# Pacing the convolution inside an attention: taps tied to sections, a later q chain, an earlier modulation vector

## The chip, the cores and the metric

The kernel runs on one core of a Trainium2 chip. The metric is the device time of one execution in microseconds (us), taken as the median of several runs. TensorE is called PE here, VectorE DVE, ScalarE ACT, GpSimd POOL and SyncE SP; SP issues nearly all DMAs.

## The reference

Two layers of a diffusion trunk, on 128 context and 512 latent tokens of width 1024. The change lies in the mixer of layer 0, which adds an attention (8 heads of 64, 2 key heads) and a convolution branch (512 channels, width 31) before one output projection:

```python
h = modulate(x, mod[0], mod[1])            # mod = silu(c) @ w_ada[l] + b_ada[l], 6 vectors a layer
q, k, v, u = split(h @ w_in)               # q, k: RMS norm, latents also rotated
att = softmax(q k^T) v                     # latents see latents and a cached context
a, gt = split(u); u = a * sigmoid(gt)      # GLU
u = silu(layernorm(depthwise_conv(u, w[31]) + bias))
x = layernorm(alpha * x + mod[2] * (concat(att, u) @ w_out))
# then FFN with mod[3..5]; layer 1 (mLSTM and FFN) likewise
```

## The kernel before

All products are fp32 split into a high and a low part, three matmuls each (L214 to L216). Tokens are 5 tiles of 128: tile 0 is context, 1 to 4 are latents.

**Ahead of the attention** the input projection runs in the order `GEMMS = "01k2qr3"`: GLU units 0 and 1 of the convolution, keys and values, GLU unit 2, two q groups ("q", "r") of four heads, GLU unit 3. Each GLU unit ends in `gated` (sigmoid `sg` on ACT, L1037; product `up` on DVE, L1041) and then `conv(i)`, the 31 taps of its 128 channels into `cy`. A tap is one DVE instruction (L1025), or a multiplication on ACT (L1030) and an addition on POOL (L1032); `CONV_DVE[i]` lists those on DVE. Taps are issued at low priority, so that a scheduler puts them where an engine is free. Each q group ends in a `chain` (L1118 to L1140) on DVE: sum of squares (L1123), some 15 instructions on 128x20 values that make a reciprocal root (L425 to L433), and scaling and rotation of 128x1024 values. Two modulation vectors for layer 0's first step are computed at the very start; `pending` holds generators of further vectors (`ada_vec`). A vector takes eight k-steps, each two loads of 256 KB and matmuls `psc<-whi,stat` and `psc<-wlo,stat`. `background()` advances them by a step. A buffer `ada_m` (L292 clears it on POOL) takes a vector's bias and result.

**The attention** is ordered by hand: 4 pairs of heads of 6 sections each, 24 sections. A section has scores of latents (`ps<-kTA,qT`), their maximum `nm` on DVE (L1218), the exponential on ACT (L1220), transposes on PE, their copies `pT` (DVE, L1266) and the products with the values (`po<-pT,vS`). In each section `modulation()` runs two k-steps of a vector while fewer than `ADA_PAIRS` have been run, and `conv_step()` counts sections (`step`). From step `NORM_AT` = 19 on, four sections in a row advance `conv_norm`: means of half the tokens (PE, then L1345 on DVE), means of the rest, variances (squares L1352 on ACT, 40 matmuls `psc<-ones,csq`, a reciprocal root on DVE), then scaling (`dg` L1368, matmuls `psc<-dg,ones`, L1373). The tanh and the rest of the swish (L1379 to L1386) are issued behind the last section. Pair 2 uses the queries of group "r" through `prep(2)`, in section 6.

**Behind it** comes `out_proj_halves` (L214 to L216), whose first PE row is that at 324.65 us below.

Of the kernel before, what the change touches and what calls it, by code (L numbers as in the profile page):

```python
# [9 lines left out]
F32 = mybir.dt.float32  # L10
# [8 lines left out]
P = 128  # L19
# [37 lines left out]
PS_F1 = (5, 3)  # L57
COMB_WHOLE = True
LATE_DVE = 0
CONV_DVE = (range(31), range(15), range(23, 31), range(8, 31))  # L60
PT_ACT = (4,)
NORM_AT = 19
CN_DVE = (1, 1)
SPLIT0 = None
LATE_AFF = (0, 1, 2, 3, 4)
LATE_LO = ()
PTOK = 8
GEMMS = "01k2qr3"
ADA_IN_ATT = 5
ADA_PAIRS = 20  # L70
FAST = (1, 3)
FIRST_DVE = ()
FIRST_HI = ((0, 0, 0), (0, 0, 1), (0, 1, 0), (0, 1, 1))
# [20 lines left out]
def trunk_kernel(ctx: ExitStack, tc: tile.TileContext, I, O):  # L94
# [17 lines left out]
    K.piece = 0  # L112
    K.pe = None
    K.ordered = False
    K.ada_group = 1
    K.tail = False

# [31 lines left out]
    def ps1(dtype=F32):  # L149
        return K.psB.tile([P, 512], dtype, name="ps1")  # L150
# [83 lines left out]
    adap = ada_scope.enter_context(tc.tile_pool(name="adap", bufs=2, side="right"))  # L234
    psc_scope = ctx.enter_context(ExitStack())
    psC = psc_scope.enter_context(tc.tile_pool(name="psC", bufs=1, space=PSUM, side="right", reuse_waits="tile"))
    K.ada_m = lambda: adap.tile([P, 256], F32, name="ada_m")

    def ring_raw():
        return tuple(f32(x) for x in ring_pair())  # L240
# [92 lines left out]
    def ada_vec(l, v):  # L333
        return ada_steps(l, [(v, 256 * j) for j in range(4)], {2: 0, 5: 1}.get(v))
# [159 lines left out]
    def out_proj_halves(w, S, finish):  # L494

        ah, al = act
        ws = load_n512(w, 0)
        pss = [ps1() for _ in range(NT)]
# [472 lines left out]

    K.startup = False
    K.ada_raw = ring_raw
    pending += [ada_vec(0, v) for v in (2, 3, 4)]

    with ExitStack() as m0s:
        m0 = m0s.enter_context(tc.tile_pool(name="m0", bufs=1, reuse_waits="tile"))
# [12 lines left out]
        if True:  # L990
# [16 lines left out]
                scalar1=0.5, scalar2=None, op0=ALU.mult)  # L1007
            S0 = PAD + SEQ + PAD

            def conv(i):  # L1010

                y = cy[:, i, :]
                with tc.high_priority(offset=-CONV_BEHIND):
                    dve = CONV_DVE[i]
                    if 0 in dve:
                        nc.vector.tensor_scalar(
                            out=y, in0=up[:, i, 0:CW], scalar1=cw[:, i, 0:1], scalar2=cols[:, 64 + i:65 + i],
                            op0=ALU.mult, op1=ALU.add)
                    else:
                        nc.scalar.activation(  # L1020
                            out=y, in_=up[:, i, 0:CW], func=AF.Identity, scale=cw[:, i, 0:1],
                            bias=cols[:, 64 + i:65 + i])
                    for k in range(1, CONV_K):
                        if k in dve:
                            nc.vector.scalar_tensor_tensor(  # L1025
                                out=y, in0=up[:, i, k:k + CW], scalar=cw[:, i, k:k + 1], in1=y,
                                op0=ALU.mult, op1=ALU.add)
                        else:
                            tp = upp.tile([P, CW], F32, name="tap", bufs=2)
                            nc.scalar.activation(  # L1030
                                out=tp, in_=up[:, i, k:k + CW], func=AF.Copy, scale=cw[:, i, k:k + 1])
                            nc.gpsimd.tensor_tensor(out=y, in0=y, in1=tp, op=ALU.add)  # L1032

            def gated(i, half, pa, pg):

# [15 lines left out]
            def glu(i, steps=2):  # L1051
                us = u_w[0] if i == 0 else u_units(i)
                for half in range(2):
                    ps = u_ps[half] if i == 0 else ps2()
                    pa, pg = ps[:, 0], ps[:, 1]
                    ks = range(4, 8) if i == 0 else range(KT)
                    fm_half(us[1], half, pg, ks)
                    fm_half(us[0], half, pa, ks)
                    background(steps)
                    gated(i, half, lambda: pa, pg)  # L1060
                conv(i)

            def glu_behind(i):
                us = u_units(i)
                for half in range(2):
                    pg = psC.tile([P, 512], F32, name="psc")
                    fm_half(us[1], half, pg)

                    def a_part():
                        pa = psC.tile([P, 512], F32, name="psc")  # L1070
                        fm_half(us[0], half, pa)
                        return pa

                    gated(i, half, a_part, pg)
                    yield
                conv(i)


            gains = cvp.tile([P, 2, HD], F32, name="gains")
# [33 lines left out]
            def chain(x, c0, n):  # L1113
# [48 lines left out]
            def q_group(grp, kn=None):  # L1162
                ws = load_n256(w_in, grp * 256)
                for t in range(NT):
# [50 lines left out]
        def exps(ps, dst, sm, multi):  # L1215

            nm = att.tile([P, 1], F32, name="nm", bufs=4)
            nc.vector.tensor_reduce(  # L1218
                out=nm, in_=ps, axis=AX.XY if multi else AX.X, op=ALU.max, negate=True)
            nc.scalar.activation(out=dst, in_=ps, func=AF.Exp, bias=nm[:, 0:1], scale=1.0, accum_out=sm)  # L1220

        def context_weights(i):

            qT, g = qTs[i], i // 2
            sp = ps2()
            pp = Ps[i, -1] = att.tile([P, 2, P], F32, name="pp")
            for h in range(2):
                for x, kT in enumerate((kTA, kTB)):
                    matmul(
# [24 lines left out]
        def turned(i, s, j):  # L1254
# [8 lines left out]
            if j in PT_ACT:  # L1263
                nc.scalar.copy(out=pT, in_=tp)
            else:
                nc.vector.tensor_copy(out=pT, in_=tp)  # L1266
            return pT

        def values(i, s, j, pT):
# [118 lines left out]
        ada_late = [(0, 5)] + [(1, v) for v in range(6)]  # L1388
# [27 lines left out]
        parts = prep(1)  # L1416
        next(parts)
        next_weights(2)
        step, norm = 0, None

        def conv_step():

# [2 lines left out]
            if step == NORM_AT:  # L1425
# [60 lines left out]
        K.ordered = False  # L1486
        K.ada_group = 1
        drain()
        for _ in norm:
            pass  # L1490
        cls.close()
    ada_scope.close()
    psum_plan(0, *PS_F0)
# [82 lines left out]
        nc.sync.dma_start(out=v_d[:, h, t], in_=tmp[:, 0:256])  # L1576

    with Sub(0) as S:
        S.rows(ALPHA)
        out_proj_halves(I["w_out_a"][0], S, S.finish_mixer("f0"))  # L1580
# [526 lines left out]
```

## Time and profile before

| | |
|---|---|
| median of 3 runs | 1729.05 us (1727.44 to 1731.74) |
| profiled execution, own time | 1731.09 us |
| its span | 1729.3 us |
| busy share in the span | PE 92%, DVE 62%, POOL 57%, ACT 46% |
| mean granted PE clock | 0.964 |

The own time is the span with what lies around it. In the rows, the granted clock is a share of full speed: 1.00 is the level of 2.4 GHz, and 0.5 that of 1.2 GHz. `[7.65 <-DVE up L1041]` behind a row means that the engine stood idle for 7.65 us before it, until that instruction ended. A matmul of plain fp32 operands leaves two records in the trace.

### The profile page before, as it was taken

To read this page: it belongs to the slowest core of one execution; us is meant where nothing else is said; L and a number is where in the kernel's file an instruction comes from. 1 tells how busy PE (TensorE), PEld (TensorE's weight loads), DVE (VectorE), ACT (ScalarE), POOL (GpSimd) and SP (SyncE) were. 2 spreads that over 40 slices of the span, in tenths; PEclk is the share of its full clock that TensorE was granted. 3 is DMA by queue.
4 is the path that set the end of the run, shared out by engine and by line. 5 is a ranking of instruction groups with operands and counts; after the bars stand their busy time and mean duration, and the time that the engine had idled before them with its cause. 6 is when DMAs were issued, how large, how long until landed. Compare 5 with 4: busy or idle time off the path is not lost. (4 is left out here: it accounts for less than half of the span.)

```text
span 1729.3 us, 26777 instructions
## 1 busy us (share of the span) xinstructions
PE 1594.5 (92%) x9931; PEld 1403.9 (81%) x9931; DVE 1071.3 (62%) x1840; ACT 798.5 (46%) x1557; POOL 980.6 (57%) x750
## 2 busy tenths in 40 slices
PE   7989689898999999999898998997989999999996
PEld 4679456687879889888788998897988989989885
DVE  2897697477434344456777778688497245344467
ACT  2235765345444344444544545555265444344343
POOL 2346622257746546548656756755459755546555
PEclk9999799798999999999999999998999999999998
DMA  9854475233653212225232322326342422213241
GB/s 304 270 161 133 140 249 149 73 106 117 214 161 101 85 62 98 75 73 195 83 106 81 101 59 88 121 73 203 115 159 79 135 86 91 93 55 98 85 149 71
DMA packets 149257, 211.71 MB, mean 122 GB/s; under 512 B 11845, under 2 KB 88873, under 8 KB 149128
## 3 DMA queue, kind: packets, MB, share of 16 engines
q1 hardware_dynamic: 148896, 209.94, 37.5%
q8 instruction: 78, 1.28, 0.3%
q14 instruction: 51, 0.42, 0.1%
q10 hardware_dynamic: 232, 0.08, 0.0%
HBM read 186.74 MB, written 23.24 MB: 121 GB/s over the span
## 5 line engine op out<-in xcount | busy, mean ns | idle before, releaser
L188 POOL TENSOR_TENSOR wlo<-raw,whi 128x512 fp32r<-128x512 f32 x366 | 503.5, 1396 | 373.2 <-ACT whi L187 367.2
L187 ACT CAST whi<-raw 128x512 fp32r<-128x512 f32 x360 | 220.1, 620 | 405.3 <-PE ps L216 192.9
L214 PE MATMUL ps<-whi,h 128*128 128x512 f32 x640 | 252.2, 396 | 6.1 <-DVE acc L819 2.9
L215 PE MATMUL ps<-wlo,h 128*128 128x512 f32 x640 | 253.7, 397 | 0.0
L216 PE MATMUL ps<-whi,h 128*128 128x512 f32 x640 | 253.3, 396 | 0.0
L215 PE MATMUL ps<-act_l,whi 128*128 128x320 f32 (+2 forms) x704 | 220.1, 313 | 5.8 <-POOL act_l L687 4.2
L214 PE MATMUL ps<-act_h,whi 128*128 128x320 f32 (+2 forms) x704 | 220.0, 315 | 4.8 <-ACT act_h L686 4.5
L216 PE MATMUL ps<-act_h,wlo 128*128 128x320 f32 (+2 forms) x704 | 218.9, 312 | 0.0
L188 POOL TENSOR_TENSOR wlo<-s,whi 128x512 fp32r<-128x512 f32 x118 | 161.6, 1374 | 80.8 <-ACT whi L187 69.7
L819 DVE TENSOR_TENSOR acc<-acc,ps 128x512 f32<-128x512 f32 x120 | 82.0, 685 | 163.5 <-PE ps L216 163.4
L214 PEld LDWEIGHTS ps<-whi,h 128*128 128x128 f32 x640 | 120.7, 189 | 36.1 <-issue 3.8
L216 PEld LDWEIGHTS ps<-whi,h 128*128 128x128 f32 x640 | 120.7, 189 | 28.3
L215 PEld LDWEIGHTS ps<-wlo,h 128*128 128x128 f32 x640 | 120.7, 189 | 27.9 <-issue 0.4
L214 PEld LDWEIGHTS ps<-act_h,whi 128*128 128x128 f32 x704 | 134.1, 191 | 10.8 <-ACT act_h L686 5.2
L215 PEld LDWEIGHTS ps<-act_l,whi 128*128 128x128 f32 x704 | 134.3, 191 | 8.9 <-POOL act_l L687 4.5
L216 PEld LDWEIGHTS ps<-act_h,wlo 128*128 128x128 f32 x704 | 134.3, 191 | 0.0
L214 PE MATMUL ps<-T_h,whi 128*128 128x320 f32 x336 | 104.3, 310 | 3.3 <-ACT pr L611 2.1
L187 ACT CAST whi<-s 128x512 fp32r<-128x512 f32 x120 | 73.3, 615 | 72.0 <-DVE s L562 44.4
L214 PE MATMUL ps<-whi,act_h 128*128 128x256 f32 (+1 forms) x340 | 104.3, 310 | 1.4 <-DVE acc L1155 0.9
L215 PE MATMUL ps<-wlo,act_h 128*128 128x256 f32 (+1 forms) x340 | 104.4, 309 | 0.0
L215 PE MATMUL ps<-T_l,whi 128*128 128x320 f32 x336 | 104.0, 309 | 0.0
L216 PE MATMUL ps<-T_h,wlo 128*128 128x320 f32 x336 | 103.9, 309 | 0.0
(460 smaller groups left out, 3999.8 us busy)
## 6 DMA issues: line engine op xcount, KB each, us to landing
raw<-in_w_ff_dram SPq DMA_DIRECT2D x128, 512.0 KB
whi<-in_w_ada_dram SPq DMA_DIRECT2D x80, 256.0 KB
wlo<-in_w_ada_dram SPq DMA_DIRECT2D x80, 256.0 KB
raw<-in_w_in_m_dram SPq DMA_DIRECT2D x32, 512.0 KB
ada_w<-in_w_ada_dram SPq DMA_DIRECT2D x32, 256.0 KB
acc_d<-acc SPq DMA_DIRECT2D x15, 512.0 KB
raw<-in_w_in_a_dram SPq DMA_DIRECT2D x12, 512.0 KB
rx<-acc_d SPq DMA_DIRECT2D x20, 256.0 KB
```

What stands on the lines that cost most here:

```text
L187: nc.scalar.copy(out=hv, in_=src)
L188: (eng or nc.gpsimd).tensor_tensor(out=lv, in0=src, in1=f32(hv), op=ALU.subtract)
L214: nc.tensor.matmul(out=out, lhsT=lh, rhs=rh, start=start, stop=False)
L215: nc.tensor.matmul(out=out, lhsT=lh, rhs=rl, start=False, stop=False)
L216: nc.tensor.matmul(out=out, lhsT=ll, rhs=rh, start=False, stop=stop)
L819: nc.vector.tensor_tensor(out=x, in0=x, in1=ps, op=ALU.add)
```

## The change

Six edits. (1) `CONV_DVE[3]` becomes `range(16, 31)`: eight taps of unit 3 go from DVE to ACT and POOL. (2) `conv` becomes a generator. The 16 ACT taps of unit 3 are issued three to a section from section 1 on, the remaining DVE taps (8 of unit 2, then 15 of unit 3) three to a section from section 6 on, each ordered behind the latest `nm`, exponential or `pT` copy (`K.anchor`); this is an order on one engine, not a wait between engines. (3) The chain of group "r" moves from the end of its projection into section 1. (4) A third `ada_m` buffer; `pending` takes four vectors ahead of the attention in place of three, and the attention four in place of five (sections 1 to 14 in place of 1 to 18). (5) The four steps of `conv_norm` are taken in sections 16, 17, 19 and 21 in place of 19, 20, 21 and 22. (6) The rows of the gate and norm (`S.rows`) load behind the first half of the output weights.

```diff
-CONV_DVE = (range(31), range(15), range(23, 31), range(8, 31))
+CONV_DVE = (range(31), range(15), range(23, 31), range(16, 31))
-NORM_AT = 19
+NORM_AT = 16
+NORM_STEPS = (16, 17, 19, 21)
+TAPS_AT = 6
+POOL_TAPS = 3
+DVE_TAPS = 3
-ADA_IN_ATT = 5
-ADA_PAIRS = 20
+ADA_IN_ATT = 4
+ADA_PAIRS = 16
...
-    K.ada_m = lambda: adap.tile([P, 256], F32, name="ada_m")
+    K.ada_m = lambda: adap.tile([P, 256], F32, name="ada_m", bufs=3)
...
-    pending += [ada_vec(0, v) for v in (2, 3, 4)]
+    pending += [ada_vec(0, v) for v in (2, 3, 4, 5)]
...
+                            if paced:
+                                behind(ins.ins, K.anchor["act"])
                             nc.gpsimd.tensor_tensor(out=y, in0=y, in1=tp, op=ALU.add)
+                    if paced or (i == 2 and k + 1 in dve):
+                        yield k
+                        paced = True
...
-                nc.vector.tensor_reduce(out=ss, in_=s1v, axis=AX.X, op=ALU.add)
+                ins = nc.vector.tensor_reduce(out=ss, in_=s1v, axis=AX.X, op=ALU.add)
+                if "dve" in K.anchor:
+                    behind(ins.ins, K.anchor["dve"])
...
-                chain(0, grp * 256, 4)
+                if grp == 0:
+                    chain(0, 0, 4)
...
-            if norm is not None and step < NORM_AT + 4:
+            if step in NORM_STEPS:
                 next(norm)
+            if step == 1:
+                chain(0, 256, 4)
+            for _ in range(POOL_TAPS if step < TAPS_AT else DVE_TAPS):
+                if step < TAPS_AT and len(acts) < 16:
+                    acts.append(next(taps[3]))
+                elif step >= TAPS_AT:
+                    if next(taps[2], None) is None:
+                        next(taps[3], None)
```

Three places show how the instructions move. The first is DVE just ahead of the attention's first latent maximum. Before, the end of the chain of group "r" (L1127 to L1140) stands around the last `up` of GLU unit 3:

```order
L1127 TENSOR_TENSOR acc_87<-acc_87,rr4_1839 128x5x256
L1128 TENSOR_TENSOR acc_87<-acc_87,gains_530 128x256
L1131 TENSOR_TENSOR qk_s1_1835<-acc_87,gsin_538 128x256 x4
L1199 TENSOR_TENSOR act_h_89<-acc_87,act_h_89 128x5x64
L1137 TENSOR_TENSOR acc_87<-acc_87,gcos_537 128x4x256
L1199 TENSOR_TENSOR act_h_89<-acc_87,act_h_89 128x5x64
L1041 SCALAR_TENSOR_TENSOR up_519<-sg_1987,ps2_1938 128x320
L1140 TENSOR_TENSOR acc_87<-acc_87,qk_s1_1835 128x4x256
L1218 TENSOR_REDUCE nm_2068<-ps2_2061 128x1
```

In the changed kernel the same stretch, from the first chain's last instruction (L1176) to that maximum (L1255), is:

```order
L1176 TENSOR_TENSOR acc_87<-acc_87,qk_s1_1708 128x4x256
L1236 TENSOR_TENSOR ptok_2028<-acc_87,ptok_2028 128x5x64
L1236 TENSOR_TENSOR ptok_2031<-acc_87,ptok_2031 128x5x64
L1075 SCALAR_TENSOR_TENSOR up_519<-sg_1968,ps2_1919 128x128
L1075 SCALAR_TENSOR_TENSOR up_519<-sg_1968,ps2_1919 128x192
L1236 TENSOR_TENSOR act_h_89<-acc_87,act_h_89 128x5x64 x2
L1075 SCALAR_TENSOR_TENSOR up_519<-sg_2021,ps2_1972 128x320
L1255 TENSOR_REDUCE nm_2057<-ps2_2050 128x1
```

All 24 instructions of the second chain are gone from here; `up` stands behind six short ones only. The second place is DVE in the middle of pair 0. Before, taps (L1025) stand between maxima and copies:

```order
L1218 TENSOR_REDUCE nm_2373<-ps2_2366 128x1
L1025 SCALAR_TENSOR_TENSOR cy_506<-up_519,cw_521,cy_506 128x655
L1235 RECIPROCAL ri_2376<-smc_2372 128x1
L1218 TENSOR_REDUCE nm_2380<-ps2_2366 128x1
L1025 SCALAR_TENSOR_TENSOR cy_506<-up_519,cw_521,cy_506 128x655
L1266 COPY pT_2411<-ps1_2406 128x512
```

Now the second chain's short instructions (L437 to L445) stand there, between the same kinds of neighbours:

```order
L1157 TENSOR_REDUCE ss4_2214<-qk_s1_2212 128x20
L437 TENSOR_SCALAR rh_v_2217<-ss4_2214 128x20
L1304 COPY pT_2259<-ps1_2254 128x512
L438 TENSOR_SCALAR rr4_2216<-rh_v_2217 128x20
L1255 TENSOR_REDUCE nm_2267<-ps2_2261 128x1
L439 TENSOR_SCALAR rr4_2216<-rr4_2216 128x20
L1304 COPY pT_2275<-ps1_2270 128x512
L442 TENSOR_TENSOR rh_a_2218<-rr4_2216 128x20
```

The chain fills sections 1 to 5; one tap is left in pair 0, 15 stand in pair 1 and 7 in pair 2. The third place is PE in section 16, the fourth of pair 2. Before, two k-steps of a modulation vector (`psc_3001<-whi`, `wlo`) stand between context scores and values:

```order
L128 MATMUL ps2_3048<-kTB_504,qT_2816 128x128
L128 MATMUL psc_3001<-whi_3068,stat_109 32x256 x2
L128 MATMUL psc_3001<-wlo_3069,stat_109 32x256 x2
L128 MATMUL psc_3001<-whi_3076,stat_109 32x256 x2
L128 MATMUL psc_3001<-wlo_3077,stat_109 32x256 x2
L128 MATMUL po_2905<-pT_3030,vS_505 64x256 x2
```

Now the first means of the convolution's norm stand there, which before came three sections later:

```order
L140 MATMUL ps2_3120<-kTB_504,qT_2898 128x128
L140 MATMUL psc_3158<-cy_506,ones_3154 128x128 x4
L140 MATMUL psc_3158<-cy_506,ones_3154 128x192 x4
L140 MATMUL po_2993<-pT_3102,vS_505 64x256 x2
L140 MATMUL po_2993<-pT_3118,vS_505 64x256 x2
```

The variances now stand behind the transposes of section 19, the scaling behind those of section 21, each with the next latents' scores ahead of it.

## Rows read from the trace of the kernel before

**Rows 1.** Head of the page.

```profile
span 1729.3 us, 26777 instructions
```

**Rows 2.** Stretches: length, busy us of each engine (instructions), clock, DMA share, GB/s.

```profile
125.50:170.40 44.90, 44.90 (x346) 44.90 (x347) 32.72 (x51) 26.64 (x52) 31.82 (x24) 0.96 0.41 131
170.40:184.50 14.10, 2.13 (x16) 1.80 (x14) 13.65 (x26) 5.47 (x11) 7.20 (x6) 0.61 0.21 71
184.50:197.30 12.80, 10.13 (x57) 6.40 (x58) 5.41 (x10) 12.03 (x24) 8.06 (x6) 0.62 0.51 164
197.30:230.00 32.70, 26.20 (x238) 17.93 (x237) 26.98 (x38) 24.78 (x51) 25.32 (x18) 0.95 0.61 193
230.00:260.00 30.00, 27.07 (x242) 17.83 (x240) 28.25 (x57) 18.08 (x38) 0.60 (x2) 0.94 0.79 277
260.00:284.50 24.50, 23.32 (x228) 15.20 (x228) 21.80 (x38) 15.27 (x37) 8.24 (x7) 1.00 0.53 175
284.50:304.20 19.70, 17.55 (x114) 14.83 (x112) 9.05 (x17) 6.88 (x14) 2.47 (x2) 0.89 0.53 102
304.20:324.60 20.40, 15.25 (x63) 9.38 (x62) 16.09 (x40) 7.09 (x14) 0.31 (x1) 0.52 0.06 17
324.60:400.00 75.40, 71.90 (x376) 60.78 (x376) 44.74 (x98) 34.61 (x79) 38.93 (x29) 0.99 0.38 125
```

**Rows 3.** Waits, 170 to 185: us in total, times, longest us.

```profile
PE ps L128 <- DVE up L1041: 7.7, 1, 7.7
PE ps L131 <- ACT qT L1210: 4.3, 1, 4.3
```

**Rows 4.** Timeline of DVE, start and duration in us.

```profile
164.70 1.49 DVE L1123 TENSOR_REDUCE ss<-qk_s 128x20 f32<-128x1280 f32 x1 [1.40 <-ACT qk_s L1121]
...
169.41 0.18 DVE L426 TENSOR_SCALAR rr<-rh_v 128x20 int32<-128x20 int32 x1
169.62 1.21 DVE L427 TENSOR_SCALAR rr<-rr 128x20 int32<-128x20 int32 x1
...
183.93 0.48 DVE L1041 SCALAR_TENSOR_TENSOR up<-sg,ps 128x320 f32<-128x320 f32 x1
184.33 1.22 DVE L1140 TENSOR_TENSOR acc<-acc,qk_s 128x1024 f32<-128x1024 f32 x1
```

**Rows 5.** Timeline of POOL in the same stretch.

```profile
166.26 10.31 POOL L1032 TENSOR_TENSOR cy<-cy,tap 128x655 f32<-128x655 f32 x7 [6.10 <-ACT tap L1030]
```

**Rows 6.** Timeline of PE at the attention's start.

```profile
176.40 0.41 PE L128 MATMUL ps<-kTB,qT 128*128 128x128 f32 x1
184.47 0.63 PE L128 MATMUL ps<-kTA,qT 128*128 128x320 f32 x1 [7.65 <-DVE up L1041]
```

**Rows 7.** Groups of DVE, pair 0, then pair 1: count, busy us, mean ns.

```profile
L1025 DVE SCALAR_TENSOR_TENSOR cy<-up,cw,cy 128x655 f32<-128x655 f32 x8 | 12.7, 1581 | 0.4 <-POOL cy L1032 0.3
...
L1025 DVE SCALAR_TENSOR_TENSOR cy<-up,cw,cy 128x655 f32<-128x655 f32 x16 | 14.3, 891 | 0.0
```

**Rows 8.** Stretch of one section's two k-steps, matmuls into `psc` alone.

```profile
200.30:201.35 1.05, 1.01 (x16) 0.42 (x16) 0.00 (x0) 0.00 (x0) 1.00 0.00 0
```

**Rows 9.** Timeline of PE in pair 3.

```profile
286.03 2.36 PE L128 MATMUL psc<-cy,ones 128*128 128x128 f32 x16
...
290.85 2.32 PE L128 MATMUL psc<-cy,ones 128*128 128x320 f32 x8
...
298.28 5.94 PE L128 MATMUL psc<-ones,csq 128*128 128x1 f32 x34 [0.26 <-ACT csq L1352]
...
309.19 2.39 PE L128 MATMUL psc<-dg,ones 128*128 128x128 f32 x8 [1.60 <-DVE dg L1368]
314.12 0.76 PE L128 MATMUL psc<-dg,ones 128*128 128x128 f32 x2 [2.54 <-DVE cy L1373]
...
324.65 0.50 PE L214 MATMUL ps<-whi,act_h 128*128 128x512 f32 x1 [0.39 <-ACT rb L1310]
```

**Rows 10.** Waits, 284 to 327.

```profile
DVE rh_v L425 <- PE psc L128: 9.6, 1, 9.6
```

More of the change, by code (lines that the diff above doesn't have):

```diff
@@ L114, in trunk_kernel, with behind @@
     K.ordered = False
+    K.anchor = {}
+    def behind(ins, anchor):
+        tc.add_manual_dep(
+            ins, anchor.name, mybir.DependencyInfo(mybir.DependencyClass.NoSync, mybir.DependencyReason.DATA),
+            reason="pace of the attention")
     K.ada_group = 1
@@ L492, in load_n512, with out_proj_halves @@
         return by_k(out, 1)
-    def out_proj_halves(w, S, finish):
+    def out_proj_halves(w, S, finish, rows):
         ah, al = act
         ws = load_n512(w, 0)
+        rows()
         pss = [ps1() for _ in range(NT)]
@@ L1008, in trunk_kernel, with conv, low @@
             S0 = PAD + SEQ + PAD
-            def conv(i):
+            def conv(i, paced=False):
                 y = cy[:, i, :]
[L1013 to L1025, printed above, removed]
+                dve = CONV_DVE[i]
+                def low():
+                    return tc.high_priority(offset=0 if paced else -CONV_BEHIND)
+                for k in range(CONV_K):
+                    with low():
+                        if k == 0 and k in dve:
+                            nc.vector.tensor_scalar(
+                                out=y, in0=up[:, i, 0:CW], scalar1=cw[:, i, 0:1], scalar2=cols[:, 64 + i:65 + i],
+                                op0=ALU.mult, op1=ALU.add)
+                        elif k == 0:
+                            ins = nc.scalar.activation(
+                                out=y, in_=up[:, i, 0:CW], func=AF.Identity, scale=cw[:, i, 0:1],
+                                bias=cols[:, 64 + i:65 + i])
+                            if paced:
+                                behind(ins.ins, K.anchor["act"])
+                        elif k in dve:
+                            ins = nc.vector.scalar_tensor_tensor(
@@ L1026, in conv @@
                                 out=y, in0=up[:, i, k:k + CW], scalar=cw[:, i, k:k + 1], in1=y,
                                 op0=ALU.mult, op1=ALU.add)
+                            if paced:
+                                behind(ins.ins, K.anchor["dve"])
                         else:
                             tp = upp.tile([P, CW], F32, name="tap", bufs=2)
-                            nc.scalar.activation(
+                            ins = nc.scalar.activation(
                                 out=tp, in_=up[:, i, k:k + CW], func=AF.Copy, scale=cw[:, i, k:k + 1])
+                            if paced:
+                                behind(ins.ins, K.anchor["act"])
@@ L1032, in conv, with start_conv @@
                             nc.gpsimd.tensor_tensor(out=y, in0=y, in1=tp, op=ALU.add)
+                    if paced or (i == 2 and k + 1 in dve):
+                        yield k
+                        paced = True
+            taps = {}
+            def start_conv(i):
+                taps[i] = conv(i, i == 3)
+                if i < 3:
+                    next(taps[i], None)
             def gated(i, half, pa, pg):
@@ L1060, in glu @@
                     gated(i, half, lambda: pa, pg)
-                conv(i)
+                start_conv(i)
             def glu_behind(i):
@@ L1075, in glu_behind @@
                     yield
-                conv(i)
+                start_conv(i)
             gains = cvp.tile([P, 2, HD], F32, name="gains")
@@ L1122, in chain @@
                 ss = smallp.tile([P, NT, n], F32, name=f"ss{n}", bufs=1)
-                nc.vector.tensor_reduce(out=ss, in_=s1v, axis=AX.X, op=ALU.add)
+                ins = nc.vector.tensor_reduce(out=ss, in_=s1v, axis=AX.X, op=ALU.add)
+                if "dve" in K.anchor:
+                    behind(ins.ins, K.anchor["dve"])
                 rr = smallp.tile([P, NT, n], F32, name=f"rr{n}", bufs=1)
@@ L1217, in exps @@
             nm = att.tile([P, 1], F32, name="nm", bufs=4)
-            nc.vector.tensor_reduce(
-                out=nm, in_=ps, axis=AX.XY if multi else AX.X, op=ALU.max, negate=True)
-            nc.scalar.activation(out=dst, in_=ps, func=AF.Exp, bias=nm[:, 0:1], scale=1.0, accum_out=sm)
+            K.anchor["dve"] = nc.vector.tensor_reduce(
+                out=nm, in_=ps, axis=AX.XY if multi else AX.X, op=ALU.max, negate=True).ins
+            K.anchor["act"] = nc.scalar.activation(
+                out=dst, in_=ps, func=AF.Exp, bias=nm[:, 0:1], scale=1.0, accum_out=sm).ins
         def context_weights(i):
@@ L1225, in context_weights @@
             sp = ps2()
-            pp = Ps[i, -1] = att.tile([P, 2, P], F32, name="pp")
+            pp = Ps[i, -1] = att.tile([P, 2, P], F32, name="pp", bufs=1)
             for h in range(2):
@@ L1265, in turned @@
             else:
-                nc.vector.tensor_copy(out=pT, in_=tp)
+                K.anchor["dve"] = nc.vector.tensor_copy(out=pT, in_=tp).ins
             return pT
@@ L1386, in conv_norm @@
                     CN_LO[i % 2].tensor_tensor(out=lo, in0=cy[:, i, c0:c0 + n], in1=f32(hi), op=ALU.subtract)
-        ada_late = [(0, 5)] + [(1, v) for v in range(6)]
+        ada_late = [(1, v) for v in range(6)]
         pending += [ada_vec(*x) for x in ada_late[:ADA_IN_ATT]]
@@ L1418, in trunk_kernel @@
         next_weights(2)
-        step, norm = 0, None
+        step, norm, acts = 0, None, []
         def conv_step():
@@ L1488, in trunk_kernel @@
         drain()
-        for _ in norm:
-            pass
+        for x in (taps[2], taps[3], norm):
+            for _ in x:
+                pass
         cls.close()
@@ L1578, in trunk_kernel @@
     with Sub(0) as S:
-        S.rows(ALPHA)
-        out_proj_halves(I["w_out_a"][0], S, S.finish_mixer("f0"))
+        out_proj_halves(I["w_out_a"][0], S, S.finish_mixer("f0"), lambda: S.rows(ALPHA))
         K.ada_m = lambda: S.fp.tile([P, 256], F32, name="ada_m")
```

## The prediction

> **What bounds the kernel now.** I first read the stretches [rows 2] for the places where PE stands still; the change touches only the first 330 us of the span of 1729.3 us [rows 1]. From 125.5 to 170.4 us PE is busy all of the 44.9 us: what is added there to PE lengthens the kernel. From 170.4 to 184.5 it works 2.13 of 14.1 us while DVE works 13.65: DVE is the bound. In pair 0 (197.3 to 230) no engine is full, but PE, DVE, POOL and ACT all work 25 to 27 of 32.7 us and hand work to each other section by section. In pair 1 DVE works 28.25 of 30 us, in pair 2 PE 23.32 of 24.5. In pair 3 (284.5 to 324.6) PE is busy 17.55 and 15.25, together 32.8 of 40.1 us, the second part at the lower clock level (0.52). From 324.6 PE is busy again, 71.9 of 75.4 us.
>
> Next the waits at the two gaps. At the start PE waits 7.7 us for DVE's last `up` [rows 3]: context scores end at about 176.8, the first latent score comes at 184.47 [rows 6]. That `up` runs only at 183.93, because the chain of group "r" stands ahead of it on DVE from 164.70 to 185.55 [rows 4]. In pair 3 DVE waits 9.6 us for the variances [rows 10] and PE afterwards 1.60 and 2.54 us for the scaling [rows 9]: norm work done in a row at the end.
>
> **The change part by part.** The sum is made against the profiled execution's own time, 1731.09 us, which is 2.0 above the median of 1729.05.
>
> *A, the fourth vector ahead of the attention: +4.0.* A section's two k-steps take 1.01 us of PE [rows 8]; eight k-steps are 4.0 us, on a PE with no gap. Bounds: +3 (their first and last matmuls overlap with the neighbours) and +9 (each k-step also waits 0.6 us for its buffer pair or its load). The loads, 16 of 256 KB or 4.2 MB, find room: this stretch moves 131 GB/s where pair 1 moves 277 [rows 2], and 44.9 us times the difference is 6.6 MB. The third `ada_m` costs nothing but one clearing on POOL (busy 31.82 of 44.9, all off PE's path); if that cover were gone, one clearing's wait, under 2 us by the pace of POOL's additions [rows 5].
>
> *B, the chain out of the start: -7.6.* With the chain gone, `up` follows six short instructions, and the first latent score can follow the context scores: 184.47 goes to about 176.9. The wait for `qT` (4.3 us, [rows 3]) stays, so the late one next is ACT, which feeds `up` with its sigmoid and casts `qT`. Bounds: -4 (ACT, in order, is held by taps that wait for POOL) and -12 (7.6 and the lower clock, under which 10.13 us of PE work stand in the stretch behind [rows 2]).
>
> *C, pair 0: +3.5.* DVE loses the eight taps (12.7 us, [rows 7]) but one, and gains the chain. The chain took 20.9 us elapsed, with seven other short pieces within (`ptok`, `act_h`, `up`), which I put at the 0.48 of the last `up`: some 17.5 us [rows 4]. DVE then has 26.98 - 12.7 + 1.6 + 17.5 = 33.4 us for a pair that lasts 32.7. At a share of 0.92, below pair 1's 0.94, that is 36.2 us. Bounds: 0 and +8. The 0 would be if the chain ran uncontended: its instructions alternate between 0.18 and 1.21 us [rows 4] while POOL adds taps at 1.47 us each [rows 5], so most of the chain's length is POOL's pace; the +8 is if each of the 15 short ones cost 1.21 and a `pT` copy stood behind it. POOL gets eight more additions and stays busy longer than pair 0.
> The Trainium skill has a rule that speaks against this place for the chain: its page "GPSIMD Engine Reference", section "1. Specifications", says that GpSimd shares its SBUF interfaces with VectorE and contends with DVE instructions that have two SBUF inputs or run in a two-port mode. The 0.18 against 1.21 agrees with it, and so do taps of 1.58 us mean in pair 0 against 0.89 in pair 1 [rows 7]. By the rule alone all the chain is contended and the pair 8 us longer; by the rows half of its short instructions are not.
>
> *D, pair 1: +1.0.* The same 15 to 16 taps (14.3 us, [rows 7]); POOL, idle there before (0.60 us), now still adds taps at its start, and each tap that meets one costs 0.7 more. Bounds -1 and +4.
>
> *E, pair 2: +2.0.* Means come in (2.36 + 2.32 = 4.7 us, [rows 9]), the k-steps of sections 15 to 18 go (four times 1.01, [rows 8]), PE being nearly full; 1.3 for DVE's subtractions, which now stand between maxima. Bounds 0 and +5.
>
> *F, pair 3: -11.5.* Of the 32.8 us of PE work 4.7 leave. The variances now have squares made a section earlier, and the reciprocal root runs under the transposes and scores of sections 20 and 21, so its 1.60 and most of the 9.6 that DVE waited go. What is late next is the second scaling, which still waits for L1373 [rows 9]: that one I leave. PE's work at its present clock is then 28.1 us, with 0.5 of wait 28.6 in place of 40.1. Bounds: -5 (only the means leave) and -16 (of 15.25 us at 0.52 about 4.5 are won by the full clock).
>
> *Load order of the output rows: 0.* PE's first output product waited for ACT, 0.39 us [rows 9], not for a load, and PE works 71.9 of 75.4 us behind it [rows 2]; if that cover failed, one row's load.
>
> Sum: 4.0 - 7.6 + 3.5 + 1.0 + 2.0 - 11.5 = -8.6. The own time goes to 1722.5, the median to **1720**.
>
> **The rivals.**
>
> *Clock follows the closed gaps: 1711.* The granted clock is 0.61 and 0.62 in the two stretches behind the first wait, 0.52 in pair 3's second part [rows 2], each time behind PE's idle stretches. If these close far enough that the upper level holds, B is -11 and F -16: 9 us more. For it: pair 2, without gaps, has 1.00. Against it: the 4.3 us wait remains at the start, and pair 3's tail is short pieces. The Trainium skill says the same of gaps ("TensorE: Matmul & The Clock Gate", section "HAM oscillation — how this bites in real kernels"): waits let the clock drop, and the next piece starts slow. The rows agree with it at both places.
>
> *DVE takes it back: 1728.* The chain, the taps and the maxima saturate DVE in pairs 0 and 1: C +8 and D +4 in place of 3.5 and 1. For it: 33.4 us of work in 32.7, DVE at 0.94 already in pair 1, and a maximum behind a contended instruction holds ACT and PE. Against it: pair 2 has slack on DVE (21.80 of 24.5), and it starts with fewer taps left.
>
> *The change does not do what it says: 1727.* If the taps of sections 6 to 13 slip by more than the two sections left before 16, the means wait for them, PE stands in pair 2, and F shrinks to -5. 1720 + 6.5 is 1727.
>
> *Loads ahead of weights: slower, 1735.* The fourth vector's loads now stand on SP's queue ahead of the second half of group "r"'s weights and of GLU unit 3's; 4.2 MB at the highest rate shown, 277 GB/s, are 15 us. If all of it showed on PE ahead of the attention, 1720 + 15 = 1735. It is slower than before once more than 8.6 of these are exposed. For it: buffer pairs are given back by PE only as it uses them, and SP issues in order. Against it: 6.6 MB of room, worked out under A.
>
> **How the numbers follow.** The forecast has 0.47 (by itself 1715 to 1726), the clock 0.18, DVE's saturation 0.14, slipped taps 0.10, late loads 0.11. About 0.3% (5 us, 1724 to 1734) is what a measurement of this kernel tells from no change. Faster: the clock, and of the forecast all but 0.03 above 1724, with some of the two cases near 1727: 0.18 + 0.44 + 0.06 = 0.68. Same: 0.03 + 0.18 + 0.01 = 0.22. Slower: 0.10. The range goes from 1708 (below the clock's case, within B and F at their ends less A's and C's spread) to 1732, which leaves out most of the late loads and the far ends.
>
> **What would show each step.** A: PE stays without gap to the last projection product, which comes 3 to 5 us later, at 173 to 175; a wait for a load there speaks for the last rival. B: under 2 us between context and first latent scores, no wait for `up`. C: chain pieces between `pT` copies, pair 0 at 35 to 37 us, DVE over 0.9. D: 30 to 32 us. E: means in pair 2 without a wait for a tap. F: about 28 us from pair 3's first scores to the first output product, no wait of DVE near 9 us. The prediction is wrong if pairs 0 and 1 grow by more than 10 us, if the means wait for taps, or if PE waits ahead of the attention for loads.

## The result and the profile after

The changed kernel takes 1741.01 us (median of 4, 1739.63 to 1743.28), the kernel before beside it 1728.3 us: a ratio of 1.0071 with a 95% interval of 1.0052 to 1.0091. The change makes the kernel slower by 0.7%; 1720 us and "faster" were forecast.

The profiled execution has an own time of 1739.63 us, 8.5 above that of before. The medians lie 12.7 apart: the traced execution of the changed kernel is the shortest of its four, and the stretches below account for the 8.5 alone. Its head:

```profile
span 1737.8 us, 26781 instructions
```

Both kernels are best cut at the same events of PE: the first transposes of `ptok` behind the projection, the first latent scores, the first transposes of pair 1's queries in section 1, the transposes of the divisors of pairs 0, 1 and 2 (`ps<-ident,rb`), and the first output product. First the kernel before between these events, in the columns of [rows 2]:

```profile
170.31:184.47 14.16, 2.19 (x17) 1.86 (x14) 13.71 (x26) 5.44 (x11) 7.29 (x6) 0.62 0.21 72
184.47:199.87 15.40, 11.79 (x69) 7.82 (x69) 7.20 (x13) 14.63 (x29) 10.45 (x8) 0.69 0.43 136
199.87:222.69 22.82, 19.68 (x192) 12.89 (x191) 17.95 (x28) 18.00 (x38) 17.87 (x14) 0.97 0.75 237
222.69:255.74 33.05, 27.69 (x238) 18.39 (x238) 31.26 (x57) 19.30 (x40) 5.66 (x5) 0.92 0.70 244
255.74:280.90 25.16, 24.02 (x235) 15.97 (x234) 23.95 (x40) 15.39 (x38) 6.75 (x5) 1.00 0.62 199
280.90:324.65 43.75, 36.36 (x208) 26.53 (x206) 27.30 (x60) 16.88 (x34) 4.27 (x5) 0.73 0.30 63
```

Then the changed kernel between the same events:

```profile
175.37:180.87 5.50, 1.62 (x16) 1.34 (x13) 2.52 (x4) 4.58 (x10) 4.48 (x5) 0.97 0.56 183
180.87:193.79 12.92, 9.96 (x69) 6.51 (x69) 6.20 (x12) 12.48 (x26) 9.61 (x8) 0.88 0.51 164
193.79:223.66 29.87, 21.84 (x194) 14.17 (x193) 28.25 (x51) 19.63 (x42) 19.90 (x14) 0.89 0.46 148
223.66:261.13 37.47, 27.67 (x236) 17.67 (x235) 34.68 (x51) 21.17 (x43) 16.90 (x11) 0.91 0.61 207
261.13:293.39 32.26, 26.52 (x213) 18.50 (x212) 29.73 (x45) 19.48 (x44) 13.41 (x8) 1.00 0.29 102
293.39:333.77 40.38, 31.89 (x166) 22.98 (x164) 25.37 (x57) 16.58 (x33) 0.00 (x0) 0.71 0.22 35
```

The reader is to see, line by line, the length and then DVE and POOL. The start is won (14.16 to 5.50, 15.40 to 12.92). Then the three stretches of pairs 0 to 2 grow by 7.1, 4.4 and 7.1 us, and in each DVE is busy 92 to 95% of the time (79, 95 and 95% before); POOL is busy 16.9 in the second where it was 5.7, and 13.4 in the third where it was 6.8. The last stretch shrinks by 3.4 only. The projection ends 5.1 us later (175.37 against 170.31). 5.1 - 8.7 - 2.5 + 7.1 + 4.4 + 7.1 - 3.4 is 9.1; behind the first output product 0.7 are won again (1404.0 us against 1404.7), within rounding the 8.5 of the span.

PE's waits show who is late. In pairs 0 and 1, first before (199.87 to 255.74), then changed (193.8 to 261.1 us; total, times, longest):

```profile
PE po L128 <- DVE pT L1266: 3.5, 3, 1.5
PE ps L131 <- DVE pT L1266: 0.9, 3, 0.4
```

```profile
PE po L140 <- DVE pT L1304: 7.5, 3, 4.7
PE ps L143 <- DVE pT L1304: 6.8, 5, 3.9
```

PE now waits 14.3 us, in place of 4.4, for copies that stand on DVE among chain instructions and taps. In the last stretch, first before, then after:

```profile
PE psc L128 <- DVE cy L1373: 2.5, 1, 2.5
PE psc L128 <- ACT csq L1352: 2.1, 4, 1.1
PE psc L128 <- DVE dg L1368: 1.6, 1, 1.6
```

```profile
PE po L140 <- DVE pT L1304: 3.3, 4, 1.6
PE psc L140 <- DVE cy L1411: 2.5, 1, 2.5
PE ps L140 <- ACT ptok L1257: 1.7, 1, 1.7
```

The waits for squares and `dg` (3.7 us) are gone but for 0.2, and are replaced by waits for copies and exponentials (5.0).

### The profile page after: what moved, and what is told of

The parts are those of the page before. It is cut to its first block, busy times and chain, and to the rows that moved or that the text cites. A ratio compares the mean times of both kernels' runs of the same rounds, so it can differ in the third digit from the quotient of the medians.

```text
span 1737.8 us, 26781 instructions
## 1 busy us (share of the span) xinstructions
PE 1600.7 (92%) x9931; PEld 1408.0 (81%) x9931; DVE 1070.2 (62%) x1832; ACT 804.7 (46%) x1565; POOL 993.5 (57%) x758
## 3 DMA queue, kind: packets, MB, share of 16 engines
q1 hardware_dynamic: 148896, 209.94, 37.4%
```

## The experiments

Three theories for the 14 to 19 us that pairs 0 to 2 lost. Theory 1, contention: DVE's instructions take longer while POOL adds taps, and the change puts more of both side by side. Theory 2: DVE simply has more work there. Theory 3: the additional taps on ACT hold the exponentials. Lengths of stretches, in us, between the events above, from each run's own trace ("pair 0" is the third line above, "last" the sixth; "front" goes from the keys' first transposes on PE to the end of the projection):

| kernel | ratio to before (95%) | front | start (two) | pair 0 | pair 1 | pair 2 | last | behind it |
|---|---|---|---|---|---|---|---|---|
| before | 1 | 44.9 | 14.2, 15.4 | 22.8 | 33.1 | 25.2 | 43.8 | 1404.7 |
| changed | 1.0071 (1.0052 to 1.0091) | 52.5 | 5.5, 12.9 | 29.9 | 37.5 | 32.3 | 40.4 | 1404.0 |
| e1 | 1.0043 (1.0027 to 1.0059) | 53.6 | 14.8, 12.7 | 19.3 | 39.6 | 33.3 | 36.3 | 1404.6 |
| e2 | 1.0071 (1.0051 to 1.0091) | 53.4 | 5.4, 14.3 | 29.7 | 35.7 | 40.3 | 38.9 | 1404.1 |
| e3 | 0.9994 (0.9976 to 1.0012) | 44.7 | 5.7, 12.3 | 28.6 | 37.0 | 25.2 | 45.2 | 1408.9 |
| e4 | 0.9998 (0.9985 to 1.0011) | 44.8 | 5.6, 14.4 | 29.9 | 36.1 | 25.2 | 43.0 | 1407.5 |
| e5 | 1.0003 (0.9988 to 1.0019) | 52.9 | 5.5, 14.0 | 25.2 | 27.6 | 32.6 | 40.2 | 1406.9 |
| e6 | 1.0207 (1.0177 to 1.0237) | 52.9 | 14.8, 14.3 | 22.0 | 37.5 | 28.6 | 42.7 | 1426.8 |
| e7 | 1.0061 (1.0038 to 1.0084) | 53.8 | 5.5, 14.6 | 29.8 | 35.6 | 29.6 | 42.9 | 1404.5 |
| e8 | 1.0015 (1.0000 to 1.0030) | 45.2 | 5.6, 15.6 | 30.9 | 35.0 | 26.8 | 44.6 | 1406.9 |
| e9 | 1.0052 (1.0038 to 1.0066) | 52.8 | 5.4, 14.0 | 29.4 | 35.6 | 32.9 | 39.1 | 1409.2 |
| e10 | 1.0003 (0.9991 to 1.0014) | 45.0 | 5.6, 14.5 | 30.4 | 37.8 | 24.5 | 44.7 | 1401.3 |
| e11 | 1.0056 (1.0037 to 1.0076) | 44.6 | 14.2, 15.3 | 22.5 | 39.9 | 26.3 | 44.1 | 1407.5 |
| e12 | 0.9973 (0.9959 to 0.9988) | 52.7 | 3.9, 13.9 | 20.4 | 32.9 | 26.7 | 43.5 | 1406.9 |
| e13 | 1.0133 (1.0098 to 1.0168) | 53.2 | 5.5, 13.9 | 29.6 | 35.5 | 26.3 | 42.5 | 1418.0 |

The times in the expectations below are on the scale of the first measurement (before 1728 us); beside the runs below the kernel before took 1731 to 1735, so the ratios count. A front that begins with fewer projection products done ahead of the keys' transposes is longer by these: in the changed kernel it is 7.6 us longer, and the projection ends 5.1 later (e12 has units and groups in another order, and there the front compares with nothing). The changed kernel also keeps `pp` in one buffer, which the six edits don't name; e3 has it too and takes the time of the kernel before.

**e1, the chain back ahead of the attention**

```diff
-                if grp == 0:
-                    chain(0, 0, 4)
+                chain(0, grp * 256, 4)
...
-            if step == 1:
-                chain(0, 256, 4)
```

> The changed kernel with the chain of group "r" back ahead of the attention. Theory 1 (contention: DVE instructions with two SBUF operands are slowed while POOL adds taps, and both now fill pairs 0 and 1): the start loses 8 to 11 us, pair 0 gets back about 6 us, pair 1 only 2 to 4, since POOL still adds taps there; about 1743 us. Theory 2 (the amount of DVE work, contention aside): pairs 0 and 1 get back all of the 14 us that they lost, about 1738 us. Theory 3 (the eight additional taps on ACT hold the exponentials): pairs 0 and 1 stay as long as they are, about 1751 us.

The start loses 9.3 us and pair 0 gets back 10.6, but pair 1 gets longer by 2.1, although DVE has no chain in it. Theory 3 as the only cause falls (the pairs did not stay). Theory 1 had the sum of pairs 0 and 1 (8.5 us back) but not the places: pair 0 runs through faster and POOL's additions, tied to sections, pile into pair 1 (POOL 22.7 us busy there, 16.9 in the changed kernel). Theory 2 wanted all of the loss back, which was 11.5 between these events; but the ratio, 1736 us on the first scale, lies nearer to its 1738 than to theory 1's 1743, since the last stretch is 4 us shorter. This run does not part the two; e5 and e11 do.

**e2, the eight taps back on DVE**

```diff
-CONV_DVE = (range(31), range(15), range(23, 31), range(16, 31))
+CONV_DVE = (range(31), range(15), range(23, 31), range(8, 31))
-TAPS_AT = 6
+TAPS_AT = 5
...
-                if step < TAPS_AT and len(acts) < 16:
+                if step < TAPS_AT and len(acts) < 8:
```

> The changed kernel with the eight taps of unit 3 back on DVE (still paced; DVE taps from section 5 on, so that 31 fit ahead of the means). Theory 1: POOL's additions end some 12 us earlier, the chain's end and the taps of pair 1 run uncontended; pairs 0 and 1 together 4 to 7 us shorter, although DVE has 7.1 us more taps; about 1736 us. Theory 2: DVE has 7.1 us more work and the kernel is 5 to 7 us slower, about 1747 us. Theory 3: ACT loses 6.7 us of taps, pairs 0 and 1 lose most of the 14 us again, about 1730 us.

All three are wrong in size. Pairs 0 and 1 win 2.0 us and pair 2 loses 8.0, where 15 taps now stand, but the last stretch is shorter by 1.5 and the ratio is the same. Eight taps more on DVE cost no more than eight additions on POOL did.

**e3, vector and norm steps back**

```diff
-NORM_AT = 16
-NORM_STEPS = (16, 17, 19, 21)
+NORM_AT = 19
+NORM_STEPS = (19, 20, 21, 22)
-ADA_IN_ATT = 4
-ADA_PAIRS = 16
+ADA_IN_ATT = 5
+ADA_PAIRS = 20
-    pending += [ada_vec(0, v) for v in (2, 3, 4, 5)]
+    pending += [ada_vec(0, v) for v in (2, 3, 4)]
```

> The changed kernel with three vectors ahead of the attention, five in it up to section 18, two ada_m buffers, and the norm's steps back in sections 19 to 22; pacing, taps and chain as changed. If the norm's steps apart save nothing (as the profile after reads: 40.4 us from pair 2's divisors to the output product against 43.8, of which 4.7 are the means that moved): the front gets 5 us shorter, pair 2 loses 4.7 and gains 3.3 to 4.0, pair 3 gains 3 to 4 back; about 1737 us. Rival (the norm's steps apart do save what was forecast, and something else covers it): pair 3 gets 10 us or more longer, about 1746 us.

All of the loss is gone: 0.9994, where about 1737 us were expected. Pair 2 is back at 25.2, 7.1 shorter, where its loss of the means and gain of k-steps had been put at about 1. The last stretch gains 4.9, about the means that return to it. The start's 11.6 us and the 9.7 of pairs 0 and 1 cancel.

**e4, the chain alone**, in the kernel before: the diff of e1 the other way round, with the chain's first instruction tied behind the latest `nm` or `pT` as in the change.

> The kernel before with the one edit that the chain of group "r" runs in section 1 on, behind the latest maximum or copy. All three theories: the start 8 to 11 us shorter. Theories 1 and 2: pairs 0 and 1 together 8 to 12 us longer, since chain and 31 taps share DVE; about 1728 us. Theory 3 (only the additional ACT taps hurt): pairs 0 and 1 at most 3 us longer, about 1720 us.

The start wins 9.6 us, pairs 0 and 1 lose 10.1: 0.9998. Theories 1 and 2 as expected; theory 3 falls for good as the only cause: there are no additional ACT taps here.

**e5, without unit 3's additions on POOL**

```diff
-                            nc.gpsimd.tensor_tensor(out=y, in0=y, in1=tp, op=ALU.add)
+                            if i < 3:
+                                nc.gpsimd.tensor_tensor(out=y, in0=y, in1=tp, op=ALU.add)
```

> The changed kernel without the 15 additions of unit 3's taps on POOL (left out; their multiplications on ACT stay, unread), so that POOL is free from the end of unit 2's taps on, early in pair 0. Contention: the chain's short instructions fall from about 0.75 us mean to 0.4, the taps of pair 1 from 1.10 to 0.89, the small ones of 1.5 us to 0.17; pairs 0 and 1 together 10 to 14 us shorter, about the time of the kernel before. Amount of work alone: DVE has the same instructions at nearly the same durations, pairs 0 and 1 at most 3 us shorter, 8 to 12 us slower than the kernel before.

Pairs 0 and 1 are 14.5 us shorter. DVE's groups, in pair 1 of the changed kernel and then of e5 (count, busy us, mean ns), each with a step of the chain in pair 0 at its end (lines of e5 below L1055 count one more):

```profile
L1044 DVE SCALAR_TENSOR_TENSOR cy<-up,cw,cy 128x655 f32<-128x655 f32 x14 | 15.4, 1100 | 0.0
L389 DVE TENSOR_SCALAR s<-modc 128x16 f32<-128x16 f32 x1 | 1.5, 1536 | 0.0
L1304 DVE COPY pT<-ps 128x512 f32<-128x512 f32 x8 | 5.5, 681 | 0.7 <-PE ps L143 0.7
...
L1167 DVE TENSOR_TENSOR qk_s<-acc,gsin 128x256 f32<-128x256 f32 x4 | 4.2, 1100 | 0.0
```

```profile
L1044 DVE SCALAR_TENSOR_TENSOR cy<-up,cw,cy 128x655 f32<-128x655 f32 x14 | 12.5, 893 | 0.0
L389 DVE TENSOR_SCALAR s<-modc 128x16 f32<-128x16 f32 x1 | 0.2, 163 | 0.0
L1305 DVE COPY pT<-ps 128x512 f32<-128x512 f32 x8 | 5.5, 683 | 0.2
...
L1168 DVE TENSOR_TENSOR qk_s<-acc,gsin 128x256 f32<-128x256 f32 x4 | 1.4, 416 | 0.0
```

The same instructions on the same operands: a tap 1100 against 893 ns, a 128x16 one 1536 against 163, a step of the chain 1100 against 416. The chain's 15 short instructions did not fall as expected, 6.3 us together in the changed kernel and 5.9 here: unit 2's additions still run beside them (POOL busy 9.5 us in pair 0). DVE's sum over the two pairs falls by 13.4 us (28.25 + 34.68 to 23.37 + 26.16 busy), which is 0.9 us for each of the 15 additions left out. DVE has the same instructions, so theory 2 falls, and theory 1 has its size.

**e11, the other way round: additions where POOL was idle**, in the kernel before

```diff
+            if 7 <= step <= 11:
+                if step == 7:
+                    K.busy = upp.tile([P, CW], F32, name="tap", bufs=2)
+                    nc.gpsimd.memset(K.busy, 0.0)
+                for _ in range(3):
+                    nc.gpsimd.tensor_tensor(out=K.busy, in0=K.busy, in1=K.busy, op=ALU.add)
```

> The kernel before with 15 additions of the size of a tap's on POOL, on an unused buffer, behind the last tap's addition, from 226 us on, where POOL was idle through pair 1; nothing waits for them but one clearing of ada_m. Contention: the taps of pair 1 go from 0.89 us to 1.5 or more while they run, each addition costs DVE some 0.9 us, pair 1 gets 7 to 11 us longer, and so does the kernel. Amount of work alone: DVE has no instruction more, the time stays within 2 us.

1.0056. Pair 1's stretch and its taps, in e11; before, 17 taps took 17.6 us in this stretch, 1033 ns each:

```profile
221.20:261.10 39.90, 28.48 (x238) 18.07 (x237) 39.30 (x55) 19.05 (x40) 29.13 (x21) 0.93 0.63 218
...
L1025 DVE SCALAR_TENSOR_TENSOR cy<-up,cw,cy 128x655 f32<-128x655 f32 x16 | 22.0, 1373 | 0.1
```

DVE has nothing more to do and is busy 39.30 us in place of 31.26; pair 1 is 6.8 longer. 15 additions cost DVE 8.0 us, some 0.5 each, less than the 0.9 expected. With e5 an addition on POOL costs DVE 0.5 to 0.9 us; what sets it between the two was not tried. A tap on DVE costs 0.89.

**e10, chain and eight taps without pacing**, in the kernel before: e4 with `CONV_DVE[3] = range(16, 31)`.

> The kernel before with the chain in section 1 and the eight taps of unit 3 on ACT and POOL, not tied to sections. With e3, which has the same but paced (and the load order), this tells what pacing does. Theory (an addition on POOL costs DVE about as much as a tap on it, 13.4 us for 15 additions in e5, so neither the eight taps nor their pace matter): the time of the kernel before within 3 us, pairs 0 to 2 together 89 to 93 us as in e3 and e4. Rival (pacing keeps maxima and copies ahead of taps and is worth something): 4 us or more slower than the kernel before.

1.0003, pairs 0 to 2 together 92.7 us, against 90.8 in e3 and 91.2 in e4. Within the 2 to 3 us that these runs resolve, neither the eight taps nor their pace matter.

**e7, norm steps back alone**: `NORM_AT` and `NORM_STEPS` as in e3, the rest as changed.

> The changed kernel with the norm's four steps back in sections 19 to 22. Theory: pair 2 loses the means (4.7 us) and DVE's subtractions (3.1 us) and is 7 to 10 us shorter, pair 3 gains 4 to 5 back, and the weight splits on POOL and ACT meet fewer taps; 3 to 6 us faster than the changed kernel, so 6 to 9 slower than before. Rival (the vector is what costs): the same time as the changed kernel, 12 us slower than before.

Pair 2 and the last stretch are 72.5 us together, 72.6 in the changed kernel: the norm's steps apart are worth nothing. The forecast of 3 to 6 us gained is a miss. With e3, which differs from e7 by the vector alone (and `ada_m`'s buffers), the vector is what costs: 0.9994 against 1.0061, 11 to 12 us.

**e6, the vector alone**, in the kernel before: the last line of e3's diff the other way round, with `ADA_IN_ATT = 4`, `ADA_PAIRS = 16`, the third `ada_m` buffer and `pp` in one buffer.

> The kernel before with the fourth vector ahead of the attention, four in it (to section 14) and the third ada_m buffer alone (the tile pp with one buffer to make room). Theory: the front 5 us longer, pair 2 (sections 15 to 18) 3 to 4 us shorter, the rest as before: 1 to 3 us slower than before. Rival (this edit is what the run with vector and norm back gained): 8 to 12 us slower.

1.0207, worse than either. To the first output product 12.1 us are lost: front, pair 1 and, against what was expected, pair 2 (28.6 us, with modulation gone from its last four sections; the run e13 below shows why). Another 22 are lost behind it, in the FFN, where the vectors that are left still run; PE's longest wait there, from 432 to 512 us:

```profile
PE psc L128 <- DMA whi<-in_w_ada_dram: 9.2, 2, 8.2
```

Before, this wait is 1.7 us. Why the loads come late there in this kernel and not in the changed one was not settled.

**e13, a fifth vector in sections 15 to 18**, norm as in e7: `ADA_IN_ATT = 5`, `ADA_PAIRS = 20`.

> The changed kernel with the norm's steps back in sections 19 to 22 (as in e7) and a fifth vector in the attention, in sections 15 to 18, so that buffer pairs are taken by modulation up to there as before, while the fourth vector stays ahead of the attention. If pair 2 is longer because the output weights' splits now start at its beginning and meet the taps: the splits start 7 to 9 us later into pair 2 again, the taps of pair 2 go from 1.44 to about 0.95 us, and pair 2 goes from 29.6 (e7) to 25 to 26 us although PE has 3.3 us more to do there; the front stays 5 to 8 us longer than before. Rival (pair 2 is longer for another reason): pair 2 at 30 us or more.

Pair 2 goes to 26.3 us. The taps in it, in e7 and then in e13, with the first splits of output weights on ACT and POOL in each:

```profile
L1044 DVE SCALAR_TENSOR_TENSOR cy<-up,cw,cy 128x655 f32<-128x655 f32 x10 | 14.4, 1435 | 0.0
262.20 1.13 ACT L199 CAST whi<-raw 128x512 fp32r<-128x512 f32 x2
262.88 3.13 POOL L200 TENSOR_TENSOR wlo<-raw,whi 128x512 fp32r<-128x512 f32 x2 [11.53 <-DMA acc<-in_x_sample_dram]
```

```profile
L1044 DVE SCALAR_TENSOR_TENSOR cy<-up,cw,cy 128x655 f32<-128x655 f32 x10 | 10.0, 996 | 0.0
279.20 0.62 ACT L199 CAST whi<-raw 128x512 fp32r<-128x512 f32 x1 [1.10 <-PE psc L140]
279.90 3.10 POOL L200 TENSOR_TENSOR wlo<-raw,whi 128x512 fp32r<-128x512 f32 x2 [29.25 <-ACT whi L199]
```

Modulation loads and weight splits take their buffers from one ring of pairs. With modulation gone from sections 15 to 18 the splits (whose second half is a subtraction on POOL) start 17 us earlier, and the ten taps of pair 2 take 4.4 us longer. In e13 the splits wait for PE's k-steps again. The same shows in e6: there the first split comes at 262.83, ahead of pair 2. The kernel as a whole is slower (1.0133), since the FFN loses 13.5 us, again with PE waiting for a modulation load (7.8 us).

**e9, rows ahead of the output weights again**

```diff
-        ws = load_n512(w, 0)
         rows()
+        ws = load_n512(w, 0)
```

> The changed kernel with the rows of gate and norm loaded ahead of the output weights again. In e6 the stretch behind the first output product was 1426.8 us against 1404.7 before, in the changed kernel 1404.0. If the load order is what saves these 22 us beside an early fourth vector: the stretch behind the first output product grows by 15 to 22 us here. Rival (the 22 us of e6 belong to how that kernel's buffer pairs fall, not to this order): it stays within 3 us of 1404, and the kernel takes the changed kernel's time, 11 to 13 us over the kernel before.

1.0052, and 1409.2 us behind the first output product: the rival. The order of these loads is not what the FFN of e6 lost.

**e8, chain in section 1 and more copies on ACT**: e4 with `PT_ACT = (2, 4)`.

> The kernel before with the chain in section 1 (as in e4) and a second pT copy of each half pair on ACT in place of DVE (eight copies of 0.68 us). If DVE is the bound of pairs 0 and 1 and ACT is not: these 3 to 6 us shorter than in e4, so 3 to 6 us faster than the kernel before. Rival (what bounds is the order of maxima, exponentials and copies, whatever the engine): the same as before.

No gain: the ratio is 1.0015, and pairs 0 and 1 take 65.9 us, in e4 66.0. DVE has six copies less in pairs 0 to 2, but the same 32 taps take longer beside POOL: two in pair 0 at 1.56 us (0.97 in e4), 13 in pair 2 at 1.08 (ten at 0.95).

**e12, the projection in another order**, in the kernel before

```diff
-GEMMS = "01k2qr3"
+GEMMS = "01kqr23"
```

> The kernel before with one edit of its own: the order of the projection is 0, 1, k, q, r, 2, 3, so that the chain of group "r" runs while PE still has two GLU units to do, and needs no place in the attention. If the chain only has to lie under other PE work, ahead of the attention: the start 7 to 11 us shorter, pair 0 as before, and unit 2's taps some 8 us later on ACT and POOL, which costs pair 1 up to 5 us; 3 to 9 us faster than the kernel before. Rival (unit 2's later additions meet the chain's and the taps' instructions for as long as they are late): the same time.

0.9973 (0.9959 to 0.9988), about 5 us faster than the kernel before and 17 faster than the changed one. The chain runs under PE's last two GLU units, the wait for `up` is gone (of PE's start only 2.5 us for `qT` are left), and pairs 0 and 1 carry no chain: 20.4 and 32.9 us. Up to the first output product 5.4 us are won.

## Why the prediction was wrong

The forecast's pairs 0 to 2 [rows 2] end 4 to 7 us later than the ones above. At its own marks, the transposes of `ptok` that start at 197.28, 229.75, 260.11 and 284.57 us before and at 191.93, 229.32, 268.43 and 295.67 in the changed kernel, pairs 0 to 2 grew by 4.9, 8.8 and 2.8 us and the last stretch shrank by 2.0. So two terms failed, D and F. Pairs 0 and 1 between these marks, first before, then changed:

```profile
197.28:229.75 32.47, 25.97 (x237) 17.70 (x234) 26.75 (x37) 24.80 (x51) 25.29 (x17) 0.95 0.61 192
229.75:260.11 30.36, 27.43 (x245) 18.18 (x244) 28.61 (x57) 18.08 (x38) 0.62 (x2) 0.94 0.79 277
```

```profile
191.93:229.32 37.39, 27.12 (x238) 17.98 (x236) 34.19 (x58) 26.18 (x53) 26.45 (x18) 0.91 0.49 160
229.32:268.43 39.11, 28.96 (x242) 18.52 (x241) 37.50 (x54) 23.78 (x47) 16.97 (x11) 0.91 0.59 203
```

**A, front: +4.0 forecast, +5.1 measured.** Right in mechanism. It was priced from two k-steps in a row; PE takes them alone or in halves. The changed kernel's PE:

```profile
128.09 0.41 PE L140 MATMUL psc<-whi,stat 128*32 128x256 f32 x2
...
129.96 0.39 PE L227 MATMUL ps<-wlo,act_h 128*128 128x256 f32 x1
...
133.07 0.62 PE L140 MATMUL psc<-whi,stat 128*32 128x256 f32 x4
133.62 0.39 PE L226 MATMUL ps<-whi,act_h 128*128 128x256 f32 x1
...
140.30 0.41 PE L140 MATMUL psc<-whi,stat 128*32 128x256 f32 x2
...
140.87 0.28 PE L1140 MATMUL po<-identr,ks 128*128 128x128 f32 x1
```

Four in a row take 1.87 us, one alone 0.57, half of one 0.55. PE waited for no load there, so the last rival did not come. The size is low even so: in the seven other runs with the vector in front the projection ends at 176.6 to 178.9 us (one execution each), in the five with the same order and no vector added at 169.2 to 171.3. That is 5 to 10 us, about the upper bound.

**B, start: -7.6 forecast, -11.1 measured.** Right, with the bound for the clock nearly all added: 0.62 and 0.69 before, 0.97 and 0.88 after.

**C and D, pairs 0 and 1: +3.5 and +1.0 forecast; +7.1 and +4.4 measured between the events above, +4.9 and +8.8 at the forecast's marks.** At these C holds in mechanism and nearly in size: DVE is busy 34.2 of 37.4 us, 33.4 of 36.2 were forecast. The step that failed is D's: POOL "still adds taps at its start, and each tap that meets one costs 0.7 more". POOL goes from 0.62 to 16.97 us busy there, with additions until 247.5 us and the first splits of weights from 261 on, and DVE from 28.61 to 37.50. Sixteen taps at 1104 ns in place of 891 are 3.4 of these 8.9 us; most of the rest is other work on SBUF that the forecast left out, three 128x16 steps (L389, L390, L392) at 1.5 us in place of 0.2 and the copy of `rb` (L1340) at 1.8 in place of 0.4. With it failed "DVE loses the eight taps" as a gain: moving a tap to POOL buys nothing (e2, e10), since the addition costs DVE 0.5 to 0.9 us and the tap 0.89. Moving the chain buys nothing either (e4): 9.6 won, 10.1 lost. The Trainium skill's page "GPSIMD Engine Reference", section "8. Key points", names contention with instructions that have two SBUF inputs or run in a two-port mode. The trace agrees for the taps (1100 against 893 ns) and a step of the chain (1100 against 416). A single-input instruction is slowed as well (L389, 1536 against 163); whether it ran in a two-port mode no run here shows. The copies from PSUM keep their 681 ns in the same stretch.

**E, pair 2: +2.0 forecast; +7.1 measured between the events above, +2.8 at the forecast's marks.** There it is right in size, but its account of what comes and goes, the means for the k-steps, is short. Not looked at was what the k-steps held back: the output weights' splits, which now run beside the taps (e13) and begin in what the forecast counts as pair 1. The vector's true price is this together with A; undone, it gives back all of the loss (e3 against e7).

**F, last stretch: -11.5 forecast; -3.4 measured between the events above, -2.0 at the forecast's marks.** e7 shows that the steps apart are worth nothing in all. The failed step is the reading of [rows 10]: "most of the 9.6 that DVE waited go". DVE waiting for PE's 20 variance products (40 records, which the section on the kernel before counts as 40 matmuls) was no stall of PE. The forecast left 0.5 us of PE's idle time here; it was 7.4 before (43.75 - 36.36) and is 8.5 after (40.38 - 31.89). PE's work fell by 4.5, the means that went to pair 2. The waits for the norm were real but small, and the DVE work of norm and swish now stands among `pT` copies that PE waits for.

Three rivals were slower than the forecast. The one in which DVE saturates had the mechanism of pairs 0 and 1: its C and D, +8 and +4, are 12 us, and 13.7 were measured at the forecast's marks (the prediction's own sign of being wrong, more than 10, came true). But it kept F whole, so it said 1728, with a chance of 0.14. Slipped taps (1727) and late loads (1735) did not come: PE waited for no tap at the means (at 284.76 and 289.63 us) and for no load in front. The measured 1741 lies beyond all three: a chain whose two ends cancel (e4), taps (e2, e10) and norm steps (e7) that change nothing, and the vector, which costs on PE in front and on DVE behind it. Two slips of arithmetic, 33.4 / 0.92 (36.3, not 36.2) and the clock's rival (7.9 us more, not 9), move none of this.

## What to carry to other kernels

Where DVE and POOL both work on SBUF, count POOL's instructions as DVE work before moving anything between them: here an addition on POOL cost DVE 0.5 to 0.9 us, and the tap itself 0.89. When work is taken out of a stretch, ask what was waiting behind it: it may come earlier and collide. A wait of one engine for the bounding engine's own work is no gain; sum the bounding engine's idle time, and move a chain to where that engine has long work of its own (e12), not among its short exchanges.

## What the hardware showed

In pair 3 the granted clock fell in a stretch in which PE showed no gap. Two stretches of the changed kernel in the columns of [rows 2], ahead of the 40 records of the variance products and over them and the values behind, and then one of the kernel before, from within its variance products:

```profile
293.39:299.20 5.81, 4.09 (x31) 3.27 (x30) 3.27 (x6) 5.61 (x11) 0.00 (x0) 1.00 0.00 0
299.20:309.00 9.80, 9.80 (x51) 8.65 (x50) 3.47 (x14) 0.97 (x3) 0.00 (x0) 0.54 0.01 2
```

```profile
301.00:304.20 3.20, 3.20 (x18) 3.19 (x17) 0.00 (x0) 0.00 (x0) 0.00 (x0) 0.50 0.18 34
```

In the changed kernel PE stood still once ahead of them, 1.72 us until 298.05, and the clock was still 1.00; over the variance products, with PE busy all the time, it went to 0.54, the 1.2 GHz level for nearly all of it. In the kernel before it had reached that level within the products too, before the waits for `dg` and `cy` behind them. The forecast put the low clock behind PE's idle stretches at both places and took the rows to agree; they do at the attention's start, where PE had waited 7.65 us [rows 6], but here the level was reached in a busy stretch. What set it off was not tried.
